# Attention output with queries on the partitions, other estimates for the order of issue, and one ring for the split activations of an FFN

## The chip, the cores and the metric

The kernel runs on one core of one Trainium2 chip. The metric is device time in microseconds (us), from the first to the last instruction of one execution with what lies around it; the time of a kernel is the median of several executions. TensorE is called PE, VectorE DVE, ScalarE ACT, GpSimd POOL, and SyncE (whose queue issues the transfers) SP.

## The reference, cut

Two layers of three residual blocks over 256 tokens of width 1024, each behind an RMSNorm: a SwiGLU feed-forward block (FFN) at half weight, a token mixer of three head groups in parallel, and a second such FFN; then a last RMSNorm.

```python
D_MODEL, SEQ, DEPTH, D_FF = 1024, 256, 2, 2816
MLA_HEADS = 6;  FOX_HEADS = 6            # 12 heads of causal attention, values of 64 channels
def swiglu(h, w_gu, w_down):
    g, u = h @ w_gu                      # two halves, D_FF each
    return (silu(g) * u) @ w_down
def hybrid_mixing(h, ...):
    z = h @ w_in
    ya = mla_mixer(...)      # low-rank q and kv, each with a norm of its own; 64 + 32 rotated channels
    yb = pool_mixer(...)     # causal means over windows of 2, 4, 8 and 16
    yc = fox_mixer(...)      # attention with c[t] - c[s] added to the scores, c = cumsum(log_sigmoid(f))
    return concat([ya, yb, yc]) @ w_out
def reference(x, ...):
    for l in range(DEPTH):
        x = x + 0.5 * swiglu(rmsnorm(x, ffn1_norm[l]), ...)
        x = x + hybrid_mixing(rmsnorm(x, mix_norm[l]), ...)
        x = x + 0.5 * swiglu(rmsnorm(x, ffn2_norm[l]), ...)
    return rmsnorm(x, final_norm)
```

## The kernel before, in words

**Products.** All of `x` stays in SBUF, transposed: channels on the partitions, 256 tokens along the free axis, 8 chunks. A product with a weight is done in three fp32r matmuls: the weight is split in a rounded half `hi` and a rest `lo`, and so is the activation (`hT` holds both halves of the normed input, chunk by chunk; `ph` and `pl` are those of an FFN's middle activation and of the mixer's output). The three are hi by hi, hi by lo and lo by hi, L230 to L232, with the weight stationary and 256 tokens moving. In the last FFN the down product is turned round, so that tokens end on the partitions: there `ph` and `pl` are stationary and the weight moves (L237 to L239). SP loads raw weights in packs of 128x1024; ACT casts them to `hi` (L328), DVE subtracts to `lo` (L343), into 8 places each.

**An FFN** has 22 blocks of 128 middle channels. Each has a gate and an up group of 24 matmuls (8 chunks by three) and a down block of 24 (8 chunks of output by three). The gate is scaled with the norm's factor `R` on DVE (L588), passes a SiLU on ACT (L592), is multiplied by up on DVE (L602), and `split_out` makes `ph` on ACT (L370) and `pl` on DVE (L373). `ffn_order` puts the down block of a middle block LAG = 2 pairs of groups behind its own; the last H = 4 down blocks stand at the end. `ph` and `pl` come from `ptile`: 8 buffers each of 288 floats, of which 256 are used, from an offset that goes round the four values of SKEW. The mixer takes its 8 pairs of output tiles `ys` from the same buffers.

**A norm** is not put ahead of its product: the product runs on unnormed `hT`, and the factor is applied behind it. The factor's chain is: squares, a sum over the partitions on PE (L452, a column per 128 tokens), DVE adds epsilon (L456), POOL takes the power -0.5 (`rsqrt`, L364), PE spreads the factor over the partitions (L465), ACT copies it to `R` (L470). Gate groups cannot leave their banks before `R` is there.

**A mixer** starts with `mix_head` (low-rank inputs and forget gates). Then, as tasks: `lowrank` (transposes, split) and `qkv` (L223 to L225, 36 matmuls); `gates`, which makes the log gates `lf` on ACT and POOL; `decay`, which sums them over time on PE (L243 on `cs` and `lf`), copies the sum to `pc`, and fills the other halves of the tiles `fqk` on DVE (L958, four per head pair); `chunks` (q and k of the fox heads, and the pooling input), with `fox_evac` (L931, L932) into `fqk`; `q_evac` with the rotation of `qf` (`rope`, L820 to L823); `mla_T`, transposes (L247) into `mt`. `attn` runs for each of six head pairs per layer: scores with queries on the partitions (L243), `softmax` on DVE and ACT, the exponentials `e` scaled by the inverse of their sums (L1025 to L1027), three transposes to `pTs`, and the weighted values with v stationary, so that the output has channels on the partitions, as `mix_out` wants it; ACT and DVE split it straight into `yh` and `yl` (L996, L1001), each head on its own half of the partitions. Three PSUM banks of eight belong to a head pair.

**The order** on each engine is fixed when the program is built. Every piece of work is a generator that yields a time (or an event, or a number of banks) and a rank; the class `Issue` keeps a clock per engine, adds an estimated duration for each instruction and LAT for each hop between engines, and lets the ready task of lowest rank go first (L141 to L157). So an estimate that changes reorders instructions everywhere.

```python
    def on(self, eng, cost, *after):      # L112: a clock of estimates, not of the chip
        t = max(self.clk[eng], self.now ...) + cost
    def rsqrt(m, n, key): ...
        return r, q.on("POOL", 0.48)
    def ptile(nm):                        # L534
        o = SKEW[turn[nm] % len(SKEW)]
        return sp.tile([P, 288], F32R, tag=nm, bufs=8, name=nm)[:, o:o + 256]
```

## Time and profile before

| | |
|---|---|
| time, median of 3 executions | 959.35 us (958.14 to 959.65) |
| the profiled execution | 959.65 us, of which the span is 957.9 us |
| PE busy | 933.4 us, 97% |
| DVE busy | 625.2 us, 65% |
| ACT busy | 502.5 us, 52% |
| POOL busy | 56.1 us, 6% |
| transfers | 54% of the 16 DMA engines' time |

The busy time of PE is drawn from the start of a matmul to its modelled end; matmuls overlap, so a busy PE need not be at its peak pace. The pace is read from the starts of the instructions in the timeline, and PE's idle time from the view of its waits, which names the line and the engine that ended each wait.

### The profile page before, as it was taken

To read this page: it belongs to the slowest core of one execution; us is meant where nothing else is said; L and a number is where in the kernel's file an instruction comes from. 1 tells how busy PE (TensorE), PEld (TensorE's weight loads), DVE (VectorE), ACT (ScalarE), POOL (GpSimd) and SP (SyncE) were. 2 spreads that over 40 slices of the span, in tenths; PEclk is the share of its full clock that TensorE was granted. 3 is DMA by queue.
4 is the path that set the end of the run, shared out by engine and by line. 5 is a ranking of instruction groups with operands and counts; after the bars stand their busy time and mean duration, and the time that the engine had idled before them with its cause. 6 is when DMAs were issued, how large, how long until landed. Compare 5 with 4: busy or idle time off the path is not lost.

```text
span 957.9 us, 18788 instructions
## 1 busy us (share of the span) xinstructions
PE 933.4 (97%) x7788; PEld 921.4 (96%) x7788; DVE 625.2 (65%) x1018; ACT 502.5 (52%) x797; POOL 56.1 (6%) x104
## 2 busy tenths in 40 slices
PE   8999999998999999999999999999989999999997
PEld 7999999997989999999999999999988999999997
DVE  6755555568996755555686555557599676555553
ACT  6544444456664644444465444445565665444442
POOL 1000000022210000000000000000504000000000
PEclk9999999999999999999999999999999999999999
DMA  7776656422463766565556566652524557555631
GB/s 258 242 256 196 193 192 188 157 86 96 144 192 109 259 199 198 198 198 185 169 170 212 192 198 198 196 178 75 173 73 140 191 160 258 196 184 194 197 113 44
DMA packets 48326, 168.95 MB, mean 176 GB/s; under 512 B 5360, under 2 KB 5744, under 8 KB 48240
## 3 DMA queue, kind: packets, MB, share of 16 engines
q1 hardware_dynamic: 48096, 167.66, 54.0%
q8 instruction: 61, 1.00, 0.4%
q14 instruction: 25, 0.20, 0.1%
q10 hardware_dynamic: 144, 0.09, 0.0%
HBM read 166.68 MB, written 1.05 MB: 175 GB/s over the span
## 4 chain that ended last, share of the span: by engine, by line
PE 84%; DVE 9%; POOL 2%; issue 1%; DMA 1%; ACT 1%; SPq 0%; POOLq 0%; DVEq 0%; ACTq 0%
PE bank L231 24%; PE bank L230 24%; PE bank L232 24%; DVE lo L343 2%; PE bank L239 2%; PE bank L237 2%; PE bank L238 2%; PE bank L243 1%; PE bank L223 1%; PE bank L225 1%; PE bank L224 1%; DVE fqk L958 1%; PE bank L247 1%; POOL rsn L364 1%; DVE sm L1012 1%
## 5 line engine op out<-in xcount | busy, mean ns | idle before, releaser
L343 DVE TENSOR_TENSOR lo<-raw,hi 128x1024 fp32r<-128x1024 f32 (+3 forms) x320 | 382.7, 1204 | 180.3 <-ACT hi L328 179.4
L230 PE MATMUL bank<-hT,hi 128*128 128x256 f32 x1536 | 430.2, 280 | 0.0
L232 PE MATMUL bank<-hT,lo 128*128 128x256 f32 x1536 | 426.4, 278 | 0.7 <-DVE lo L343 0.4
L231 PE MATMUL bank<-hT,hi 128*128 128x256 f32 x1536 | 426.2, 277 | 0.0
L328 ACT CAST hi<-raw 128x1024 fp32r<-128x1024 f32 (+3 forms) x320 | 328.6, 1030 | 161.1 <-PE bank L231 105.1
L232 PEld LDWEIGHTS bank<-hT,lo 128*128 128x128 f32 x1536 | 289.4, 188 | 1.5 <-DVE lo L343 1.5
L230 PEld LDWEIGHTS bank<-hT,hi 128*128 128x128 f32 x1536 | 289.5, 188 | 0.7 <-ACT hi L328 0.4
L231 PEld LDWEIGHTS bank<-hT,hi 128*128 128x128 f32 x1536 | 289.5, 188 | 0.3
L230 PE MATMUL bank<-ph,hi 128*128 128x256 f32 x656 | 183.8, 280 | 0.0
L231 PE MATMUL bank<-pl,hi 128*128 128x256 f32 x656 | 182.6, 278 | 0.8 <-DVE pl L373 0.8
L232 PE MATMUL bank<-ph,lo 128*128 128x256 f32 x656 | 182.2, 278 | 0.0
L231 PEld LDWEIGHTS bank<-pl,hi 128*128 128x128 f32 x656 | 123.2, 188 | 1.1 <-DVE pl L373 1.0
L230 PEld LDWEIGHTS bank<-ph,hi 128*128 128x128 f32 x656 | 123.3, 188 | 0.1
L232 PEld LDWEIGHTS bank<-ph,lo 128*128 128x128 f32 x656 | 123.2, 188 | 0.0
L592 ACT ACTIVATE s<-s 128x256 f32<-128x256 f32 x88 | 36.5, 418 | 150.7 <-DVE s L588 150.7
L588 DVE TENSOR_TENSOR s<-bank,R 128x256 f32<-128x256 f32 x88 | 37.2, 424 | 39.0 <-PE bank L232 36.2
L373 DVE TENSOR_TENSOR pl<-p,ph 128x256 fp32r<-128x256 f32 x88 | 37.2, 425 | 37.7 <-ACT ph L370 37.7
L370 ACT CAST ph<-p 128x256 fp32r<-128x256 f32 x88 | 35.6, 407 | 27.8 <-DVE p L602 27.6
L237 PE MATMUL bank<-lo,ph 128*128 128x256 f32 x176 | 49.3, 280 | 0.0
L239 PE MATMUL bank<-hi,ph 128*128 128x256 f32 x176 | 49.2, 280 | 0.0
L238 PE MATMUL bank<-hi,pl 128*128 128x256 f32 x176 | 49.2, 279 | 0.0
L364 POOL TENSOR_TENSOR rsn<-m,mhalf 128x2 f32<-128x2 f32 x6 | 9.2, 1536 | 642.1 <-DVE m L456 642.1
(143 smaller groups left out, 755.6 us busy)
## 6 DMA issues: line engine op xcount, KB each, us to landing
raw<-wpk SPq DMA_DIRECT2D x294, 512.0 KB, 4.1
raw<-wpk SPq DMA_DIRECT2D x16, 403.0 KB, 3.1
raw<-wpk SPq DMA_DIRECT2D x4, 288.0 KB, 3.7
x<-xin SPq DMA_DIRECT2D x4, 256.0 KB, 5.6
raw<-wpk SPq DMA_DIRECT2D x4, 256.0 KB, 5.7
out<-h SPq DMA_DIRECT2D x4, 256.0 KB, 2.2
raw<-wpk SPq DMA_DIRECT2D x2, 384.0 KB, 4.2
cs<-cst SPq DMA_DIRECT2D x1, 582.0 KB, 6.7
```

The lines of the kernel that those rows point to most:

```text
L230: T.matmul(o, lhsT=hi, rhs=xh, start=start, stop=False, skip_group_check=True)
L231: T.matmul(o, lhsT=hi, rhs=xl, start=False, stop=False, skip_group_check=True)
L232: T.matmul(o, lhsT=lo, rhs=xh, start=False, stop=stop, skip_group_check=True)
L237: T.matmul(o, lhsT=lh, rhs=rl, start=start, stop=False, skip_group_check=True)
L238: T.matmul(o, lhsT=ll, rhs=rh, start=False, stop=False, skip_group_check=True)
L239: T.matmul(o, lhsT=lh, rhs=rh, start=False, stop=stop, skip_group_check=True)
L328: A.copy(h[:, :w], r[:, :w])
L343: V.tensor_tensor(out=lo[:, :w], in0=r[:, :w], in1=h[:, :w].bitcast(F32), op=ALU.subtract)
L370: A.copy(dh, src)
L373: V.tensor_tensor(out=dl, in0=src, in1=dh.bitcast(F32), op=ALU.subtract)
L588: V.tensor_tensor(out=s, in0=b[:, 0:256], in1=g.nm.R, op=ALU.mult)
L592: A.activation(s, s, AF.Silu)
```

## The change

**The weighted values are turned round.** In `attn` the transposed exponentials are now stationary and 64 columns of v move, so that queries are on the partitions of the output. The sums' inverse is taken in a task of its own (`inverse`) and applied to the output in one DVE product of 128x256, in place of the scaling of the exponentials ahead of their transposes. Two transposes bring the scaled output `y` back to channels on the partitions, into the free half of the same bank, and `split_out` splits it, both heads in one instruction per engine.

**Estimates.** PE's fp32r rate 2245 in place of 2185, LAT 0.2 in place of 0.15, POOL's power 1.4 in place of 0.48 for two columns and other POOL costs, 0.42 for a fill (L958), and the end of an exponential 0.9.

**LAG** is 3 in place of 2. **The ring:** `ph` and `pl` of a block lie side by side in one of 8 places behind `hT`, in one tile `hb`, taken from the last place to the first; the place used by blocks 0, 8 and 16 is moved on by SKEW = 12 floats. `ys` uses the same places.

```diff
-LAG = 2
+LAG = 3
-SKEW = [28, 16, 16, 16]
+RING = 8
+SKEW = 12
-    LAT = 0.15
+    LAT = 0.2
-        return q.on("PE", 3 * 256 / 2185.0)
+        return q.on("PE", 3 * 256 / 2245.0)
...
-    hT = cp.tile([P, KC, 2, 256], F32R, name="hT")
+    hb = cp.tile([P, (KC + RING) * 512 + 64], F32R, name="hb")
+    hT = hb[:, 0:KC * 512].rearrange("p (k s t) -> p k s t", k=KC, s=2)
...
-        return r, q.on("POOL", 0.48)
+        return r, q.on("POOL", 1.4 if n > 1 else 0.55)
...
-    def ptile(nm):
-        o = SKEW[turn[nm] % len(SKEW)]
-        turn[nm] += 1
-        return sp.tile([P, 288], F32R, tag=nm, bufs=8, name=nm)[:, o:o + 256]
+    def ring(n):
+        n = RING - 1 - n % RING
+        o = (KC + n) * 512 + (SKEW if n == RING - 1 else 0)
+        return hb[:, o:o + 256], hb[:, o + 256:o + 512]
...
-        ph, pl = ptile("ph"), ptile("pl")
+        ph, pl = ring(fc)
...
-            self.ys = [(ptile("ph"), ptile("pl")) for _ in range(8)]
+            self.ys = [ring(n) for n in range(8)]
...
-        q.on("POOL", 0.4)
+        q.on("POOL", 1.3)
-        t = q.on("POOL", 0.55)
+        t = q.on("POOL", 1.3)
-        t = max(t, q.on("POOL", 0.7))
+        t = max(t, q.on("POOL", 0.35))
...
-                    t = dve(256, fast=True)
+                    t = q.on("DVE", 0.42)
...
         for h in range(2):
             yield res[h][0], R_ATT
             pt = res[h][1]
-            c0 = h * 256
-            mm(o[:, c0:c0 + 256], v[:, 0, j * P:(j + 1) * P], pt[:, 0:256], True, False)
-            t = mm(o[:, c0 + P:c0 + 256], v[:, 1, j * P:(j + 1) * P], pt[:, 256:384], False, True)
+            for tb in range(2):
+                w = slice(tb * P + 64 * h, tb * P + 64 * h + 64)
+                for k in range(tb + 1):
+                    c0 = (tb + k) * P
+                    t = mm(o[:, w], pt[:, c0:c0 + P], v[:, k, j * P + 64 * h:j * P + 64 * h + 64], k == 0, k == tb)
         g.ev_att[n].set(t)
         yield t + LAT, R_EVAC
+        y = sp.tile([P, 256], F32, tag="y", bufs=2, name="y")
+        V.tensor_tensor(out=y.rearrange("p (a d) -> p a d", a=4), in0=o[:, 0:256].rearrange("p (a d) -> p a d", a=4),
+                        in1=rc.rearrange("p a h -> p (a h)").unsqueeze(2).to_broadcast([P, 4, 64]), op=ALU.mult)
+        t = dve(256)
+        yield t + LAT, R_TP
+        for tb in range(2):
+            t = tr(o[:, 256 + tb * P:256 + (tb + 1) * P], y[:, tbs(tb)])
+        yield t + LAT, R_EVAC
         yh, yl = g.ys[c]
-        for h in range(2):
-            r = slice(64 * h, 64 * h + 64)
-            A.copy(yh[r], o[r, h * 256:(h + 1) * 256])
-            t = act(256)
-        yield t + LAT, R_EVAC
-        for h in range(2):
-            r = slice(64 * h, 64 * h + 64)
-            V.tensor_tensor(out=yl[r], in0=o[r, h * 256:(h + 1) * 256], in1=yh[r].bitcast(F32), op=ALU.subtract)
-            t = dve(256)
+        t = yield from split_out(yh, yl, o[:, 256:512])
         q.give(o, t + LAT)
...
-        t = act(384, acc=0.3)
-        yield t + LAT, R_CHAIN
-        rc = small(2, "rc")
-        V.reciprocal(rc, sums)
-        V.tensor_scalar(out=e[:, 0:P], in0=e[:, 0:P], scalar1=rc[:, 0:1], scalar2=None, op0=ALU.mult)
-        V.tensor_scalar(out=e[:, P:384], in0=e[:, P:384], scalar1=rc[:, 1:2], scalar2=None, op0=ALU.mult)
-        t = q.on("DVE", 0.67)
+        t = q.on("ACT", 0.9)
+        q.spawn(inverse(rc, sums, t + LAT))
         yield t + LAT, R_TP
...
+    def inverse(rc, sums, t):
+        yield t, R_EVAC
+        V.reciprocal(rc, sums)
+        q.on("DVE", 0.08)
```

What the estimates and the turned values do to the order is seen at three places. In the rows below a line number is followed by the operation, out<-in, the tile's shape, and a count where the same stands several times in a row; lines of the kernel after are one to three higher.

PE at the start of layer 0's second FFN, from the sum of squares (`sf`) to the spreading of the factor (`rsn`), before:

```order
L452 MATMUL bank_74<-one,sf 128x1 x2
L230 MATMUL bank_69<-hT,hi_3687 128x256
L231 MATMUL bank_69<-hT,hi_3687 128x256
L232 MATMUL bank_69<-hT,lo_3752 128x256
...
L465 MATMUL bank_71<-fs,rsn 128x128 x2
```

The same place after:

```order
L454 MATMUL bank_67<-one,sf 128x1 x2
L231 MATMUL bank_71<-hb,hi_3621 128x256
L232 MATMUL bank_71<-hb,hi_3621 128x256
L233 MATMUL bank_71<-hb,lo_3686 128x256
...
L231 MATMUL bank_71<-hb,hi_3644 128x256
L232 MATMUL bank_71<-hb,hi_3644 128x256
L233 MATMUL bank_71<-hb,lo_3716 128x256
L467 MATMUL bank_70<-fs,rsn 128x128 x2
```

Between the two stand nine matmuls of a first gate group before, and eighteen after.

DVE in layer 0's mixer, from the first decay fills (L958, `fqk`) to the first rotation (L823, `qf`), before:

```order
L958 TENSOR_SCALAR fqk_2738<-pc,cs 64x256 x2
L958 TENSOR_SCALAR fqk_2739<-pc,cs 64x256 x2
L219 TENSOR_SCALAR qf<-bank_67,lr_2614 128x288
L931 TENSOR_TENSOR fqk_2738<-bank_69,R 64x256
L932 TENSOR_TENSOR fqk_2738<-bank_69,R 64x256
L958 TENSOR_SCALAR fqk_2758<-pc,cs 64x256 x2
L958 TENSOR_SCALAR fqk_2759<-pc,cs 64x256 x2
L820 TENSOR_TENSOR r_2774<-qf,cs 128x192
L821 TENSOR_TENSOR r_2775<-qf,cs 128x6x16
L822 TENSOR_TENSOR r_2775<-qf,cs 128x6x16
L823 TENSOR_TENSOR qf<-r_2774,r_2775 128x6x32
```

The same place after, where the fills are L960, the rotation ends at L825, and `mt` is the copy behind the MLA transposes:

```order
L220 TENSOR_SCALAR qf<-bank_67,lr_2624 128x288
L822 TENSOR_TENSOR r_2728<-qf,cs 128x192
L823 TENSOR_TENSOR r_2729<-qf,cs 128x6x16
L824 TENSOR_TENSOR r_2729<-qf,cs 128x6x16
L825 TENSOR_TENSOR qf<-r_2728,r_2729 128x6x32
L960 TENSOR_SCALAR fqk_2749<-pc,cs 64x256 x2
L960 TENSOR_SCALAR fqk_2750<-pc,cs 64x256 x2
L212 COPY mt_2773<-bank_72 96x512
L933 TENSOR_TENSOR fqk_2749<-bank_71,R 64x256
L934 TENSOR_TENSOR fqk_2749<-bank_71,R 64x256
L933 TENSOR_TENSOR fqk_2750<-bank_73,R 64x256
L934 TENSOR_TENSOR fqk_2750<-bank_73,R 64x256
```

The first rotation stood behind eight of the twelve fills and one product of a fox chunk, and stands ahead of them all.

PE in layer 0's mixer around the decay sum (`cs`, `lf`), before, where L223 to L225 on `qkh` and `qkl` are the low-rank projections:

```order
L230 MATMUL bank_74<-hT,hi_2572 128x256
L231 MATMUL bank_74<-hT,hi_2572 128x256
L232 MATMUL bank_74<-hT,lo_2641 128x256
L243 MATMUL bank_68<-cs,lf_86 128x256
L243 MATMUL bank_68<-cs,lf_87 128x128
L223 MATMUL bank_73<-lo_2694,qkh 128x288
L224 MATMUL bank_73<-hi_2623,qkl 128x288
L225 MATMUL bank_73<-hi_2623,qkh 128x288
```

The same place after, where the projections are L224 to L226:

```order
L226 MATMUL bank_68<-hi_2628,qkh 128x384
L224 MATMUL bank_70<-lo_2642,qkh 128x384
L225 MATMUL bank_70<-hi_2628,qkl 128x384
L226 MATMUL bank_70<-hi_2628,qkh 128x384
L231 MATMUL bank_73<-hb,hi_2502 128x256
L232 MATMUL bank_73<-hb,hi_2502 128x256
L233 MATMUL bank_73<-hb,lo_2531 128x256
L244 MATMUL bank_74<-cs,lf_86 128x256
L244 MATMUL bank_74<-cs,lf_87 128x128
L231 MATMUL bank_73<-hb,hi_2502 128x256
```

The decay sum stood ahead of the 36 matmuls of the projections, behind a fox chunk, and stands behind them, inside the next chunk.

## Rows read from the trace of the kernel before

**Rows 1.** Page parts 1 and 2: engine totals; granted clock in 40 slices.

```profile
PE 933.4 (97%) x7788; PEld 921.4 (96%) x7788; DVE 625.2 (65%) x1018; ACT 502.5 (52%) x797; POOL 56.1 (6%) x104
...
PEclk9999999999999999999999999999999999999999
```

**Rows 2.** Waits of PE: line waited for: us in total, times, longest.

```profile
PE bank L465 <- POOL rsn L364: 4.0, 4, 1.4
PE bank L247 <- DVE qf L823: 3.4, 2, 1.7
PE bank L243 <- POOL lf L806: 2.7, 2, 1.4
PE bank L247 <- ACT pTs L209: 1.4, 2, 0.7
...
PE bank L243 <- DVE pl L1001: 0.8, 2, 0.4
PE bank L247 <- DVE e L1027: 0.8, 2, 0.4
PE bank L231 <- DVE pl L373: 0.8, 1, 0.8
```

**Rows 3.** Timeline, PE, first FFN: start us, drawn us, line, operation, operands.

```profile
28.23 0.28 PE L230 MATMUL bank<-hT,hi 128*128 128x256 f32 x1
...
31.05 0.28 PE L230 MATMUL bank<-ph,hi 128*128 128x256 f32 x1
...
33.87 0.28 PE L230 MATMUL bank<-hT,hi 128*128 128x256 f32 x1
...
39.31 0.28 PE L230 MATMUL bank<-ph,hi 128*128 128x256 f32 x1
...
42.14 0.28 PE L230 MATMUL bank<-hT,hi 128*128 128x256 f32 x1
...
47.59 0.28 PE L230 MATMUL bank<-ph,hi 128*128 128x256 f32 x1
...
50.31 0.28 PE L230 MATMUL bank<-hT,hi 128*128 128x256 f32 x1
```

**Rows 4.** Timeline, PE, second FFN, after its norm.

```profile
323.99 0.28 PE L230 MATMUL bank<-ph,hi 128*128 128x256 f32 x1
...
326.81 0.28 PE L230 MATMUL bank<-hT,hi 128*128 128x256 f32 x1
```

**Rows 5.** Timeline, PE, last FFN, where `ph` and `pl` are stationary.

```profile
843.01 0.28 PE L237 MATMUL bank<-lo,ph 128*128 128x256 f32 x1
...
845.73 0.28 PE L230 MATMUL bank<-hT,hi 128*128 128x256 f32 x1
...
851.39 0.28 PE L237 MATMUL bank<-lo,ph 128*128 128x256 f32 x1
...
854.22 0.28 PE L230 MATMUL bank<-hT,hi 128*128 128x256 f32 x1
...
856.95 0.28 PE L230 MATMUL bank<-hT,hi 128*128 128x256 f32 x1
```

**Rows 6.** Chain of waits, layer 0's mixer: start us, us, what, count.

```profile
238.74 1.84 PE bank L247 x15
240.58 3.93 PE bank L243 x24
```

**Rows 7.** Timeline, PE, norm ahead of the mixer: narrow fp32 matmuls.

```profile
203.29 0.28 PE L452 MATMUL bank<-one,sf 128*128 128x1 f32 x2
...
205.93 0.38 PE L465 MATMUL bank<-fs,rsn 128*128 128x128 f32 x2
```

**Rows 8.** Timeline, DVE, layer 0's mixer; in brackets the idle time before.

```profile
222.06 0.42 DVE L958 TENSOR_SCALAR fqk<-pc,cs 64x256 f32<-64x256 f32 x1 [2.30 <-ACT pc L209]
...
230.44 0.69 DVE L211 COPY mt<-bank 96x512 f32<-96x512 f32 x1
```

**Rows 9.** Windows, start: stretch, us, busy (count) of five engines, clock, DMA, GB/s.

```profile
18.00:21.00 3.00, 2.98 (x16) 2.99 (x17) 1.58 (x3) 2.24 (x5) 0.00 (x0) 0.60 0.90 288
```

More of the change, by code (lines that the diff above doesn't have):

```diff
@@ L197, in trunk, with dve @@
         q.free.append((0.0, ps.tile([P, 512], F32, tag=f"bank{i}", name=f"bank{i}")))
-    def dve(n, *after, fast=False):
-        return q.on("DVE", 0.07 + n / (1920.0 if fast else 960.0), *after)
+    def dve(n, *after):
+        return q.on("DVE", 0.07 + n / 960.0, *after)
     def act(n, *after, acc=0.0):
@@ L225, in mm3 @@
         T.matmul(o, lhsT=lh, rhs=rh, start=False, stop=stop)
-        return q.on("PE", 3 * int(np.prod(rh.shape[1:])) / 2185.0, *after)
+        return q.on("PE", 3 * int(np.prod(rh.shape[1:])) / 2245.0, *after)
     def mmw(o, hi, lo, xh, xl, start, stop):
@@ L239, in mm3w @@
         T.matmul(o, lhsT=lh, rhs=rh, start=False, stop=stop, skip_group_check=True)
-        return q.on("PE", 3 * 256 / 2185.0)
+        return q.on("PE", 3 * 256 / 2245.0)
     def mm(o, lhsT, rhs, start, stop, *after):
@@ L529, in final @@
             nc.sync.dma_start(out[tb, :, c], h)
-    turn = {"ph": 0, "pl": 0}
-    def ptile(nm):
-        o = SKEW[turn[nm] % len(SKEW)]
-        turn[nm] += 1
-        return sp.tile([P, 288], F32R, tag=nm, bufs=8, name=nm)[:, o:o + 256]
+    def ring(n):
+        n = RING - 1 - n % RING
+        o = (KC + n) * 512 + (SKEW if n == RING - 1 else 0)
+        return hb[:, o:o + 256], hb[:, o + 256:o + 512]
     class F:
@@ L774, in lowrank_rms @@
         G.tensor_scalar(out=g.lr[tb], in0=rs, scalar1=r, scalar2=None, op0=ALU.mult)
-        g.ev_r[tb].set(q.on("POOL", 0.2) + LAT)
+        g.ev_r[tb].set(q.on("POOL", 0.3) + LAT)
     def gates(g, tb, bB, t):
@@ L977, in attn @@
         res = [[Ev(), None], [Ev(), None]]
+        rc = small(4, "rc", bufs=3).rearrange("p (a h) -> p a h", a=2)
         for h, b in ((0, b0), (1, b1)):
@@ L980, in attn @@
             t = mm(b[:, P:384], qt[0:kk, h, P:256], kt[0:kk, h, :], True, True)
-            q.spawn(softmax(b, t, scale, res[h]))
+            q.spawn(softmax(b, t, scale, res[h], rc[:, :, h]))
             yield t, R_ATT
```

2 lines of the change are left out of this document (1 added, 1 removed).

## The prediction

> **What bounds the kernel now.** I read the page first. TensorE (PE) is busy 933.4 of 957.9 us [rows 1], so any gain is either PE time without work, which is 24.5 us in all, or matmuls that follow each other more closely. Then I read who PE waits for [rows 2]. A row there is total idle, number of waits, longest wait. Three kinds matter: four waits for the factor of a norm (`rsn`, from GpSimd), one for the first `pl` of an FFN, and ten inside the two mixers. Idle is counted from the drawn end of a matmul; a matmul is drawn 0.28 us long while the next one starts 0.113 us after it [rows 3], so a wait costs 0.17 us more than its row says. Last I read start times, because the mean duration of a matmul doesn't show its pace. The profiled execution took 959.65 us for a span of 957.9 us; the median of the runs is 959.35, 0.3 less. The sum is made as gains on the profiled execution and taken off the median.
>
> **The pace of the matmuls.** Each row of [rows 3] is the first of 24 matmuls in a row (one gate or up group, or one down block). The group at 28.23 takes 2.82 us, the down block at 31.05 takes 2.82, the two groups after it 5.44 together, the block at 39.31 takes 2.83, and the block at 47.59 takes 2.72. So there are two paces, 2.72 and 2.82 us per 24, while the granted clock is at its higher level throughout [rows 1]. What goes with them is where the moving operand lies. In the built program all halves of `hT` start 64 bytes past a multiple of 256. The `ph` and `pl` buffers are 1,152 bytes apart, so they alternate between 64 and 192, and every fourth is pushed on by 48 more bytes. The block at 39.31 is a 192, that at 47.59 a 64, that at 31.05 a 112. A 64 after a fast group is fast; a 192 is slow; after a 112 or a 192 the next group is fast again. The pace also sticks: the block at 323.99 is a 64 in a slow stretch and takes 2.82 [rows 4].
>
> **The ring.** All ring places lie at 64, as `hT` does, but the one for down blocks 0, 8 and 16 of an FFN, which lies at 112. For FFNs 1 to 3: before, eight blocks in a row lie at 112, 192, 64, 192, 240, 64, 192, 64; at 0.10 to 0.11 us for each that isn't 64 (the 240 is between, 0 to 0.11) that is 0.4 to 0.5 per eight, 1.35 per FFN of 22 blocks. After, three blocks cost 0.10 each: gain 1.05 per FFN, 3.2 for three. The slow stretch after each norm ends at down block 0, which now comes one pair of groups later: 2 x 0.10 x 3 = 0.6 lost. The output projection of the mixers reads the same buffers, much broken up by attention: 0.3 gained. In the last FFN `ph` and `pl` are the stationary operand. There a 64 at 843.01 takes 2.72, the two groups after it 5.66, the next 64 at 851.39 takes 2.83, and only the group after that, at 854.22, is fast again with 2.73 [rows 5]. With nearly all blocks at 64 this would go on in pairs: two groups slowed (0.22) for one fast block (0.11), 0.1 lost per pair of blocks, half of ten pairs if the 112s break the series: 0.5 lost. Sum: 3.2 - 0.6 + 0.3 - 0.5 = **2.4 us gained**; ends 0 and 4.
>
> **Norms.** PE puts matmuls between the sum of squares (L452) and the matmul that spreads the factor (L465). The planner now charges 1.4 instead of 0.48 for the GpSimd power, and the order has 9 more matmuls there at each of the four FFN starts (3 to 12, 9 to 18, 9 to 18; 6 to 15 in the last). The four waits cost 4.0 + 4 x 0.17 = 4.7 [rows 2]; 9 matmuls cover 9 x 0.114 = 1.03 each: **4.0 gained**, ends 3.0 and 4.7. No work is added: these matmuls stood behind the wait. What is then late is the chain factor, gate, up, `pl`, first down block. LAG 3 puts 48 more matmuls (5.5 us) ahead of that block, so the one wait for `pl` (0.8 + 0.17) goes as well: **1.0 gained**, ends 0.5 and 1.0.
>
> **Mixers, what is added.** Each of 12 head pairs gets two transposes; 15 take 1.84 us in the chain [rows 6], so 24 take 2.9. The weighted values become six 64-column fp32 matmuls, 12 records, instead of four matmuls in 8 records, which take 8/24 of 3.93 = 1.31 [rows 6]. No 64-column fp32 matmul is in the trace. Four records of one column are drawn over 0.50, four of 128 columns over 0.60 [rows 7]; less 0.17 of drain that is 0.08 and 0.11 each, 1.0 to 1.3 for 12. I take no change, as for 128 columns, with -0.3 per pair as the other end. The VectorE work that is dropped (scaling the exponentials) and that is added (scaling the output, one row-wide product) is not on PE; it counts only by the waits below.
>
> **Mixers, what is moved.** The five kinds of wait in [rows 2] (`qf`, `lf`, `pTs`, `pl` L1001, `e`) sum to 9.1, ten waits, 10.8 with 0.17 each. By the new order: (1) The wait for `lf` goes: the decay matmuls now stand behind all 36 matmuls of the low-rank projections instead of ahead of them, more than 4 us of cover for 1.4. (2) The wait for `qf` goes: VectorE does both rotations first and the eight decay fills (L958) after, 2 x 1.70 us [rows 8] that were ahead of the second. (3) A new one appears: the first scores need, after the decay matmuls, a copy on ScalarE, four fills (1.70), a copy of `mt` (0.69) [rows 8] and four products of the fills' shape (1.70 again), with hops 4.8; PE has 24 matmuls and 8 transposes in between, 3.7: wait 1.1. (4) A transpose of the second MLA pair needs a bank that VectorE frees behind four maxima: 0.7 as I follow the queues. (5) The first output scaling stands behind a weight split on VectorE: 0.2. Behind that I find each chain covered, since VectorE has 0.7 us less to do per head. With 0.3 for what I missed: 2.3 per layer, 4.6 in all; ends 1 and 11. Gain 10.8 - 4.6 - 2.9 = **3.3 us**, ends 8 gained and 3 lost.
>
> **Sum:** 2.4 + 4.0 + 1.0 + 3.3 = 10.7; 959.35 - 10.7 = **948.6 us**.
>
> **Rivals.** (a) *The waits move.* Each head pair's end is now longer by a scaling, two transposes and a split, holding its PSUM bank, so the mixers may wait as long as before: 10.8 stay. For it: the estimates say little about banks. Against: the stalls of [rows 2] all have their releaser moved ahead in the queues. Then 2.4 + 4.0 + 1.0 - 2.9 = 4.5: 954.8.
> (b) *The place of the operand does nothing* and the two paces come from something else that went along with it. Then the ring's 2.4 is 0: 951.0. Against: [rows 3] repeat with the buffers, 39.31 and 47.59 being neighbours of one loop. [...]
> (c) *Slower: the slow pace sticks.* Without the 192s, only the three 112s of an FFN can end a slow stretch. If a 112 does not, every FFN from its norm on runs like 323.99 [rows 4]: 66 groups x 0.10 = 6.6 us for each of three FFNs, 19.8, less the 5.6 lost there before (1.35 in the down blocks, 0.5 ahead of the first), 14.2 worse: 959.35 - 8.3 + 14.2 = 965.3. It decides the sign once some 70% of the groups are slow. For it: [rows 4]. Against: in [rows 3] the 112 at 31.05 comes from slow groups and leaves fast ones.
> [...]
>
> **Chances and range.** Forecast 0.62, (a) 0.15, (b) 0.08, (c) 0.05, (d) 0.10. The range 943.5 to 954.5 leaves out (c), half of (a) and a part of (d). A measurement of this kernel can tell about 0.2%, 1.9 us, from no change: all but (c) and the far end of (a) are faster by more: faster 0.93, same 0.03, slower 0.04.
>
> **What would show it.** Norms: the row L465 for `rsn` under 0.8 in all, no wait for `pl` before the first down block. Ring: down blocks of 2.72 in FFNs 1 to 3 but for numbers 0, 8 and 16; in the last FFN pairs of slow groups. Mixers: no waits for `lf` or `qf`, one of about 1 us for `fqk`. I would be wrong above all if groups of 2.82 fill an FFN, or if PE's waits in a mixer sum to more than 5 us.

## The result, and the profile after

The kernel after takes 945.15 us (median of 4, 944.66 to 945.8) where the kernel before took 958.75 in the same comparison (4 runs, 958.0 to 959.65): a ratio of 0.9856, interval 0.9844 to 0.9867. The gain is 13.6 us by the medians, 15.0 between the two profiled executions (959.65 and 944.66) and 15.9 between their spans (957.9 and 942.0); what lies around the span grew from 1.8 to 2.7 us. The forecast was 948.6, a gain of 10.7.

Page part 1 of the kernel after, as in [rows 1]:

```profile
PE 929.1 (99%) x7860; PEld 920.9 (98%) x7860; DVE 608.6 (65%) x972; ACT 497.6 (53%) x783; POOL 62.4 (7%) x104
```

PE is busy 4.3 us less in a span that is 15.9 shorter: its idle time fell from 24.5 to 12.9 us. The waits of PE after, columns as in [rows 2]:

```profile
PE bank L248 <- DVE fqk L934: 1.6, 2, 0.8
...
PE bank L248 <- ACT e L1026: 0.7, 4, 0.2
...
PE bank L467 <- POOL rsn L366: 0.3, 1, 0.3
```

The row for the norms' factor fell from 4.0 to 0.3; only the first FFN's norm still waits. The rows for `lf`, `qf`, `pTs`, `pl` and for the scaled `e` are gone. New are 0.8 per mixer for `fqk` and four short waits for `e`, now released by ACT. Behind the first norm the clock does not drop in this execution; the window that answers to [rows 9], same columns:

```profile
18.00:21.00 3.00, 2.92 (x25) 2.93 (x26) 2.37 (x4) 2.44 (x5) 0.02 (x1) 1.00 0.89 277
```

The granted clock was 0.60 there before, and is 1.00. Last the pace. The timeline of PE in the first FFN after, each row the first of 24 matmuls as in [rows 3]; the down block at 33.61 is number 0, at 112, the one at 41.87 is number 1, at 64:

```profile
33.61 0.28 PE L231 MATMUL bank<-hb,hi 128*128 128x256 f32 x1
...
36.41 0.28 PE L231 MATMUL bank<-hb,hi 128*128 128x256 f32 x1
...
41.87 0.28 PE L231 MATMUL bank<-hb,hi 128*128 128x256 f32 x1
...
44.59 0.28 PE L231 MATMUL bank<-hb,hi 128*128 128x256 f32 x1
```

2.80 us for the 112, 5.46 for the two groups behind it, and 2.72 for the 64. The whole span by stages, from each norm's sum (L452, in after L454) to the next, from the starts in both traces: the first three FFNs are 4.1, 3.6 and 2.7 us shorter, the two mixers 2.5 and 3.0, the last FFN 0.0; matmuls that the new order moved across a boundary are counted back (1.1 us of each mixer's head, 2.0 between the second and the third FFN). The sum is 15.9.

### The profile page after: what moved, and what is told of

Read it like the earlier page. It is cut to its first block, busy times and chain, and to the rows that moved or that the text cites. A ratio compares the mean times of both kernels' runs of the same rounds, so it can differ in the third digit from the quotient of the medians.

```text
span 942.0 us, 18948 instructions
## 1 busy us (share of the span) xinstructions
PE 929.1 (99%) x7860; PEld 920.9 (98%) x7860; DVE 608.6 (65%) x972; ACT 497.6 (53%) x783; POOL 62.4 (7%) x104
## 4 chain that ended last, share of the span: by engine, by line
PE 95%; DVE 2%; ACT 1%; issue 1%; DMA 1%; POOL 0%; SPq 0%; POOLq 0%; DVEq 0%
PE bank L231 26%; PE bank L233 26%; PE bank L232 26%; PE bank L244 3%; PE bank L238 2%; PE bank L240 2%; PE bank L239 2%; PE bank L248 2%; PE bank L224 2%; PE bank L225 2%; PE bank L226 2%; DMA x<-xin 1%; DVE fqk L960 0%; PE bank L467 0%; DVE fqk L934 0%
## 5 line engine op out<-in xcount | busy, mean ns | idle before, releaser
L231 PE MATMUL bank<-hb,hi 128*128 128x256 f32 x2192 | 613.7, 280 | 0.0
L233 PE MATMUL bank<-hb,lo 128*128 128x256 f32 x2192 | 608.1, 277 | 0.6 <-DVE lo L345 0.5
L232 PE MATMUL bank<-hb,hi 128*128 128x256 f32 x2192 | 607.7, 277 | 0.0
L231 PEld LDWEIGHTS bank<-hb,hi 128*128 128x128 f32 x2192 | 413.0, 188 | 0.5 <-ACT hi L330 0.2
L233 PEld LDWEIGHTS bank<-hb,lo 128*128 128x128 f32 x2192 | 411.8, 188 | 1.5 <-DVE lo L345 1.5
L232 PEld LDWEIGHTS bank<-hb,hi 128*128 128x128 f32 x2192 | 411.9, 188 | 0.3
L375 DVE TENSOR_TENSOR hb<-p,hb 128x256 fp32r<-128x256 f32 x88 | 37.2, 425 | 37.6 <-ACT hb L372 37.5
L372 ACT CAST hb<-p 128x256 fp32r<-128x256 f32 x88 | 35.4, 406 | 26.4 <-DVE p L604 26.0
L238 PE MATMUL bank<-lo,hb 128*128 128x256 f32 x176 | 49.1, 279 | 0.0
L239 PE MATMUL bank<-hi,hb 128*128 128x256 f32 x176 | 49.0, 278 | 0.0
L240 PE MATMUL bank<-hi,hb 128*128 128x256 f32 x176 | 49.0, 278 | 0.0
L604 DVE TENSOR_TENSOR p<-bank,s 128x256 f32<-128x256 f32 x88 | 36.5, 419 | 11.2 <-PE bank L233 10.2
L238 PEld LDWEIGHTS bank<-lo,hb 128*128 128x128 f32 x176 | 33.1, 188 | 0.0
L240 PEld LDWEIGHTS bank<-hi,hb 128*128 128x128 f32 x176 | 33.1, 188 | 0.0
L239 PEld LDWEIGHTS bank<-hi,hb 128*128 128x128 f32 x176 | 33.0, 188 | 0.0
```

What stands on the lines that cost most here:

```text
L231: T.matmul(o, lhsT=hi, rhs=xh, start=start, stop=False, skip_group_check=True)
L232: T.matmul(o, lhsT=hi, rhs=xl, start=False, stop=False, skip_group_check=True)
L233: T.matmul(o, lhsT=lo, rhs=xh, start=False, stop=stop, skip_group_check=True)
L238: T.matmul(o, lhsT=lh, rhs=rl, start=start, stop=False, skip_group_check=True)
L239: T.matmul(o, lhsT=ll, rhs=rh, start=False, stop=False, skip_group_check=True)
L240: T.matmul(o, lhsT=lh, rhs=rh, start=False, stop=stop, skip_group_check=True)
```

## The experiments

Each kernel was timed beside the kernel before on the same chip; the median of before lay between 958.75 and 959.64, so ratios are compared. After has 0.9856. Differences by the spans are between the two profiled executions.

### The ring

**ring_192**: all places of the ring 128 bytes further.

```diff
-        o = (KC + n) * 512 + (SKEW if n == RING - 1 else 0)
+        o = (KC + n) * 512 + 32 + (SKEW if n == RING - 1 else 0)
```

> The kernel after, with every place of the ring moved by 128 bytes: seven places lie at 192 past a multiple of 256, the eighth at 240; the order of issue and the work are the same. Theory 'place' (the pace of a matmul is set by where its moving operand lies): in the kernel before, the down block at 39.31 lay at 192 and took 2.83 us where the 64 at 47.59 took 2.72, so 22 blocks of each of three FFNs lose 0.1 each, 6.6 us, less 0.9 that the nine 112s lose already: about 5.5 us slower than after, 950.7. The mixers could gain part of it, 2 us at most, since their slow stretch at 272 to 300 us of the trace of after would be broken by 192s. So 948.5 to 951. Theory 'place does nothing': within 0.5 us of 945.15.

950.18 us (949.34 to 950.42), ratio 0.9899 (0.9884 to 0.9914): 4.1 us slower than after. PE in the first FFN, a down block at 192, the group behind it, and the start of the next:

```profile
41.60 0.28 PE L231 MATMUL bank<-hb,hi 128*128 128x256 f32 x1
...
44.43 0.28 PE L231 MATMUL bank<-hb,hi 128*128 128x256 f32 x1
...
47.16 0.28 PE L231 MATMUL bank<-hb,hi 128*128 128x256 f32 x1
```

2.83 for the block and 2.73 for the group. The work and the order are those of after, so where the operand lies does count, and rival (b) falls. The mixers' slow stretch was not broken up; their part of the expectation did not come.

**ring_no_skew**: all places at 64.

```diff
-SKEW = 12
+SKEW = 0
```

> The kernel after, with SKEW = 0: all eight places at 64. 'Place': the nine down blocks at 112 become fast, 0.09 us each, 0.8 us gained in FFNs 0 to 2. 'Sticky' (a slow stretch ends only at a place other than 64): a stretch that a wait turned slow has nothing left to end it; in the mixers the slow stretch of after ran from 272 to the next norm at 300 us, 0.108 us per 24 matmuls, and would begin earlier; where an FFN begins slow it stays so, 66 groups, 7 us. In after FFNs 0 and 1 begin fast without help, so 944.4 without stickiness in FFNs, 951 to 958 if one or two FFNs stay slow. 'Place does nothing': 945.15.

Six runs: 940.69, 940.87, 946.43, 954.65, 956.39, 957.15. One program, one order, and 16 us between its runs, while after stays within 1.1 in its four. All six count here, since the scatter is what is tested; the granted clock does not account for it, since it was 0.996 in the run of 940.87 and in that of 956.39. The profiled run (954.65) has two of its first three FFNs slow from end to end, and the third fast. PE in the first FFN, a group and a down block, then a group in the third:

```profile
40.78 0.28 PE L231 MATMUL bank<-hb,hi 128*128 128x256 f32 x1
...
43.60 0.28 PE L231 MATMUL bank<-hb,hi 128*128 128x256 f32 x1
...
46.43 0.28 PE L231 MATMUL bank<-hb,hi 128*128 128x256 f32 x1
...
497.71 0.28 PE L231 MATMUL bank<-hb,hi 128*128 128x256 f32 x1
...
500.43 0.28 PE L231 MATMUL bank<-hb,hi 128*128 128x256 f32 x1
```

2.82 and 2.83 us in the first FFN, 2.72 in the third, with every `hT`, `ph` and `pl` at 64 in both. The pace is a state that sticks: in these two FFNs, which have no odd place, nothing ended it, and each is 7 us longer for it. So the state that rival (c) feared is real. The best of these runs is 4 us faster than after, whose nine 112s in the first three FFNs cost 0.8 us in all. Where the rest lies isn't shown, since that run has no trace; the profiled run has 2.6 us less of slow pace than after in the mixers and the last FFN.

**no_ring**: after with the buffers of before.

```diff
-        ph, pl = ring(fc)
+        ph, pl = ptile("ph"), ptile("pl")
-            self.ys = [ring(n) for n in range(8)]
+            self.ys = [(ptile("ph"), ptile("pl")) for _ in range(8)]
-        y = sp.tile([P, 256], F32, tag="y", bufs=2, name="y")
+        y = sp.tile([P, 512], F32, tag="dx", bufs=3, name="y")[:, 0:256]
```

> The kernel after with the ph and pl buffers of before (8 of each, 1,152 bytes apart, at 112, 192, 64, 192, 240, 64, 192, 64) in place of the ring; the scaled output y lies in the buffers of dx for lack of room. LAG, estimates, turned values as in after. 'Place': by the starts of the matmuls the ring gave 5.1 us in FFNs 0 to 2, took 2.0 in the two mixers and 1.0 in the last FFN, so this kernel is 2.1 us slower than after: 947.3. 'Place does nothing': 945.15.

946.87 us (946.33 to 949.13), ratio 0.987 (0.9856 to 0.9885): 1.3 us slower than after, with intervals that overlap, so the times alone don't show a gain. The spans of the profiled runs differ by 2.6 us (944.54 and 941.96).

**ring_alone**: before with the ring.

```diff
-        ph, pl = ptile("ph"), ptile("pl")
+        ph, pl = ring(fc)
-            self.ys = [(ptile("ph"), ptile("pl")) for _ in range(8)]
+            self.ys = [ring(n) for n in range(8)]
```

> The kernel before with the ring alone (LAG 2, old estimates, old attention). If the ring is worth what its account in the trace says, and that doesn't hang on the other parts: 2.1 us faster than before, 956.6. 'Sticky': in before each FFN began in a slow stretch behind the wait for its norm, until the first down block at 112 ended it; here the first down block lies at 112 too, so it should end there: no loss. If a 112 does not end it: 6.6 us for each FFN, up to 970. 'Place does nothing': 958.75.

957.47 us (ten runs, 955.79 to 962.11), ratio 0.9989 (0.9973 to 1.0004): 1.1 us by the ratio, no difference that can be told. The profiled run (961.78) has most of its second FFN slow, behind the waits that the old order still has. PE there: a group, down block 8 (at 112), and the next group; then the group behind down block 16, which is at 112 too:

```profile
379.50 0.28 PE L231 MATMUL bank<-hb,hi 128*128 128x256 f32 x1
...
382.32 0.28 PE L231 MATMUL bank<-hb,hi 128*128 128x256 f32 x1
...
385.14 0.28 PE L231 MATMUL bank<-hb,hi 128*128 128x256 f32 x1
...
452.97 0.28 PE L231 MATMUL bank<-hb,hi 128*128 128x256 f32 x1
...
455.69 0.28 PE L231 MATMUL bank<-hb,hi 128*128 128x256 f32 x1
```

2.82 and 2.82, and the group at 385.14 is as slow; but the group behind block 16 takes 2.72. Of the five 112s in the first three FFNs of this trace that came in a slow stretch, three ended it (block 0 in the first and in the third FFN, block 16 here) and two did not (blocks 0 and 8 here). So a 112 ends a slow stretch often, not always.

### Estimates, turned values, LAG

**estimates_alone**: before with the new estimates only.

```diff
-    LAT = 0.15
+    LAT = 0.2
-        return r, q.on("POOL", 0.48)
+        return r, q.on("POOL", 1.4 if n > 1 else 0.55)
-                    t = dve(256, fast=True)
+                    t = q.on("DVE", 0.42)
...
```

> The kernel before with the new estimates alone (LAT 0.2, 2245, the POOL costs, 0.42 for a fill); LAG 2, old buffers, old attention. The order then has 9 to 9 more matmuls inside the norms of the four FFNs, as in after. Theory 'order' (most of the gain is waits that the new order covers): the waits for the norms' factor (4.7 us with what a wait costs beside its row) and the low clock behind the first of them (1.2) go, and so do those for lf and qf in the mixers (7.0 in four waits by the starts of the matmuls); new waits for fqk, about 1 per mixer, come. 10 us faster than before, 949 where before is 959.2. Theory 'attention' (the mixers' waits went because the turned attention leaves DVE 0.7 us less work per head): the mixers keep their waits and only the norms gain, 6 us: 953.

959.7 us (ten runs, 957.85 to 963.02), ratio 1.0008 (0.9998 to 1.0019). Neither forecast came: no gain at all. The waits of PE:

```profile
PE bank L247 <- DVE fqk L932: 4.3, 2, 2.2
PE bank L247 <- DVE e L1026: 3.3, 4, 1.5
PE bank L230 <- ACT ph L370: 1.5, 1, 1.5
PE bank L247 <- ACT pTs L209: 1.4, 2, 0.8
```

The rows for the norms, `lf` and `qf` did go, as foretold. But 1.5 us came back ahead of a first down block, and in the mixers the waits for `fqk` and for the scaled `e` grew to 4.3 and 3.3. With `pTs` that is 9.0, where the five kinds of [rows 2] sum to 9.1: the mixers wait as long as before, under other names. The granted clock fell behind them; the window of the first mixer (columns as in [rows 9]):

```profile
235.00:242.00 7.00, 6.42 (x27) 5.57 (x27) 4.26 (x9) 3.69 (x11) 0.00 (x0) 0.54 0.25 77
```

0.54, where after has 1.00 in the same stretch: fp32 matmuls of 256 columns that took 0.22 us each took 0.43 there, about twice as long. Over whole runs it was 0.985 to 0.991 in these ten, and 0.995 to 0.997 in the runs of before beside them. The mixers were 3.1 and 2.4 us longer than before, with the matmuls that the order moved ahead of them counted back, and used up what the FFNs gained.

**turned_alone**: before with the new `attn`, `softmax` and `inverse`, y in the buffers of dx; estimates, LAG and buffers of before.

```diff
-            mm(o[:, c0:c0 + 256], v[:, 0, j * P:(j + 1) * P], pt[:, 0:256], True, False)
-            t = mm(o[:, c0 + P:c0 + 256], v[:, 1, j * P:(j + 1) * P], pt[:, 256:384], False, True)
+                    t = mm(o[:, w], pt[:, c0:c0 + P], v[:, k, j * P + 64 * h:j * P + 64 * h + 64], k == 0, k == tb)
...
```

> The kernel before with the turned attention alone (queries on the partitions of the output, two transposes more per head pair, scaling of the output; y in the buffers of dx), old estimates, LAG 2, old buffers. 'Order': 24 transposes at 0.11 add 2.6 us; the waits for pTs, pl and e (0.84, 0.31, 0.31 and 0.58 per mixer beyond a matmul's pace, 4.1 in both) may go with the shorter VectorE queue; from 1.5 us faster to 2.6 slower, taken 0.5 slower than before. 'Attention': 4 us faster or more.

954.19 us (953.44 to 954.47), ratio 0.9943 (0.9927 to 0.996): 5.5 us faster than before, more than either end of the first theory. The waits of PE:

```profile
PE bank L465 <- POOL rsn L364: 4.1, 4, 1.4
PE bank L247 <- DVE qf L823: 3.4, 2, 1.7
PE bank L243 <- POOL lf L806: 2.7, 2, 1.4
```

What the order makes stayed (4.1, 3.4, 2.7, as in [rows 2]); what the attention makes (`pTs`, `pl`, `e`) is gone, and the two mixers are 2.8 us shorter each by the starts, the new transposes counted in.

**scaled_early**: after with the exponentials scaled on DVE ahead of their transposes, and y a plain copy.

```diff
-        q.spawn(inverse(rc, sums, t + LAT))
+        yield t + LAT, R_CHAIN
+        rc = small(2, "rc")
+        V.reciprocal(rc, sums)
+        V.tensor_scalar(out=e[:, 0:P], in0=e[:, 0:P], scalar1=rc[:, 0:1], scalar2=None, op0=ALU.mult)
+        V.tensor_scalar(out=e[:, P:384], in0=e[:, P:384], scalar1=rc[:, 1:2], scalar2=None, op0=ALU.mult)
+        t = q.on("DVE", 0.67)
...
-        V.tensor_tensor(out=y.rearrange("p (a d) -> p a d", a=4), in0=o[:, 0:256].rearrange("p (a d) -> p a d", a=4),
-                        in1=rc.rearrange("p a h -> p (a h)").unsqueeze(2).to_broadcast([P, 4, 64]), op=ALU.mult)
+        V.tensor_copy(y, o[:, 0:256])
```

> The kernel after with the exponentials scaled by the inverse of their sums on DVE ahead of their transposes, as before; the output is copied to y unscaled, so that PE, ACT and the way of the output (values turned, two transposes, split) stay as in after; DVE has 0.6 us more per head, in the chain from the exponentials to the transposes. Theory 'chain' (the mixers gained because that chain became shorter): waits for e come back, 0.7 us in four waits in after against 3.3 in four in the kernel with the estimates alone, with what they bring in pace and clock: 3 to 6 us slower than after, 948 to 951, ratio 0.989 to 0.992. Theory 'output' (they gained because the output's split is shorter and its bank comes free sooner): within 1 us of after, ratio 0.985 to 0.987.

956.84 us (ten runs, 952.64 to 961.1), ratio 0.9979 (0.9958 to 1.0): 11.8 us slower than after by the ratio, 8.0 by the spans of the profiled runs (950.0 and 942.0). The two mixers are 3.8 and 4.4 us longer, the rest is as in after. The clock is part of it: over whole runs it was 0.993 in the three shortest (952.64 to 952.82, the profiled one among them), 0.983 to 0.985 in the four longest (958.67 to 961.1), and 0.996 to 0.998 in after. The chain decides, not the output, and it decides more than either theory had. The waits of PE:

```profile
PE bank L248 <- DVE fqk L934: 4.3, 2, 2.2
PE bank L248 <- ACT pTs L210: 1.7, 2, 0.8
```

The waits came back under other names than I had expected. In both kernels a transpose of `qf` needs the bank that the second product of `fox_evac` (L934) frees at 231.5. PE around it, first after, then scaled_early (start us, drawn us, line, operation, count, idle before and what ended it):

```profile
229.20 0.91 PE L248 MATMUL bank<-fs,e 128*128 128x128 f32 x4
...
230.27 0.44 PE L248 MATMUL bank<-fs,e 128*128 128x128 f32 x2 [0.16 <-ACT e L1026]
...
231.52 0.64 PE L248 MATMUL bank<-fs,qf 128*96 128x128 f32 x4 [0.81 <-DVE fqk L934]
```

```profile
231.44 0.64 PE L248 MATMUL bank<-fs,qf 128*96 128x128 f32 x4 [2.16 <-DVE fqk L934]
...
231.96 1.36 PE L248 MATMUL bank<-fs,e 128*128 128x128 f32 x6
```

In after PE puts six transposes of `e` ahead of it, which need only ACT's exponentials, and waits 0.81. In scaled_early these transposes wait for DVE, which is busy with four heads' maxima and the fox product until 231.4 and then scales; they come after 231.96, and PE stands still for 2.16. What this run can't part is the shorter chain from the order that goes with it, since the planner puts the transposes in another place when the scaling stands ahead of them.

**lag2**: after with LAG = 2.

```diff
-LAG = 3
+LAG = 2
```

> The kernel after with LAG = 2. If the third pair is what covers the chain from the norm's factor to the first pl: the factor is spread 9 matmuls later than before, so the first down block waits 1 to 2 us at each FFN whose norm waits cover nothing more, 1 to 4 us slower than after (946 to 949). If the chain was covered anyway: the same as after within 0.5 us.

948.38 us (947.33 to 955.54), ratio 0.9901 (0.9864 to 0.9939): 4.3 us slower by the ratio, 3.8 by the spans. One wait came back, in the second FFN, and behind it the clock (window as in [rows 9]):

```profile
PE bank L231 <- ACT hb L372: 1.9, 1, 1.9
```

```profile
305.00:316.00 11.00, 8.98 (x62) 8.59 (x61) 9.19 (x13) 7.58 (x11) 0.00 (x0) 0.84 0.85 288
```

1.9 us of wait and 11 us at a clock of 0.84; the second FFN is 4.1 us longer than in after. One of the four runs took 955.54 at a clock of 0.993 and pulls the ratio up; it has no trace, and a slow FFN as in ring_no_skew would be of that size. The other three lie between 947.33 and 949.14. So the third pair of groups covers the chain from the norm's factor to the first `ph`, which starts later now that the factor is spread later.

**power_048**: after with the old estimate for POOL's power.

```diff
-        return r, q.on("POOL", 1.4 if n > 1 else 0.55)
+        return r, q.on("POOL", 0.48)
```

> The kernel after with the old estimate, 0.48, for POOL's power alone. The order has 3, 9, 9 and 10 matmuls inside the FFNs' norms, as before. 'Order': four waits of 1 us come back, 4.7, and the low clock behind the first norm, 1.2; FFNs then start at the slow pace behind a wait, until the 112 of the first down block: 0.5 each. 6 us slower than after, 951. If the wait only moves to another place of the chain (the gate group cannot leave its bank before the factor anyway): under 2 us.

948.46 us (947.7 to 951.65), ratio 0.9892 (0.9874 to 0.9911): 3.5 us slower. The norms' waits came back in full:

```profile
PE bank L467 <- POOL rsn L366: 4.8, 6, 1.4
```

Six waits, 4.8 us, in place of one of 0.3: four in the FFNs and two at the mixers' norms, where before had none. The low clock behind the first norm is back too (window as in [rows 9]):

```profile
18.00:21.00 3.00, 3.00 (x17) 3.00 (x18) 2.05 (x3) 2.17 (x5) 0.00 (x0) 0.63 0.95 303
```

The slow starts that I expected with them did not come: the three FFNs have no more of the slow pace than in after. And the mixers have 1.2 us less each in the sum of matmul intervals that is used in the next section, which is about the 2.5 us by which I missed. The run is not about the FFNs' norms alone: this estimate also counts in the mixers, where the order changed, the wait for `fqk` is gone, and `e` waits 2.2 us where after has 0.7.

### The two operands

**kick_192**: the odd place at 192, and read last in each closing pass of a mixer.

```diff
-SKEW = 12
+SKEW = 32
-            self.ys = [ring(n) for n in range(8)]
+            self.ys = [ring(n + 1) for n in range(8)]
```

> The kernel after with the ring's one odd place at 192 in place of 112 (SKEW 32), and with the mixers' output tiles taken one place on, so that the odd place is read last in each of the four passes at the end of a mixer; nothing else is changed. 'Sticky' (a stretch that became slow stays slow until an operand at another place ends it, and a 192 ends it each time, as in ring_192): the slow stretch from 272 to 300 us in each mixer is ended by the first pass, 1.0 us gained per mixer, the FFNs stay as they are, 2 us faster than after: 943.1 where after is 945.15, ratio 0.9836 to before. 'Place does nothing': the same as after, ratio 0.9856.

Eight runs, median 945.04: five from 943.97 to 945.26, three from 950.79 to 957.11; ratio 0.9888 (0.9846 to 0.9929). No gain that can be told, and a scatter like that of ring_no_skew is back. In the profiled run the closing stretch of the first mixer is fast; its block of 24, then the one that answers to it in after:

```profile
275.78 0.28 PE L231 MATMUL bank<-hb,hi 128*128 128x256 f32 x1
...
278.50 0.28 PE L231 MATMUL bank<-hb,hi 128*128 128x256 f32 x1
```

```profile
274.85 0.28 PE L231 MATMUL bank<-hb,hi 128*128 128x256 f32 x1
...
277.68 0.28 PE L231 MATMUL bank<-hb,hi 128*128 128x256 f32 x1
```

2.72 against 2.83, 0.9 us over that mixer, as the theory had it. The second mixer kept its slow stretch and is 1.5 us longer than in after, and the first FFN 1.0 us longer: in both the granted clock dropped where after has 1.00, with PE in the same order and behind waits as short. The window behind the first norm (as in [rows 9]), then the one in the second mixer:

```profile
18.00:21.00 3.00, 3.00 (x20) 3.00 (x19) 1.81 (x3) 1.93 (x5) 0.02 (x1) 0.64 0.91 274
690.00:695.00 5.00, 3.88 (x20) 2.98 (x21) 3.73 (x12) 3.60 (x13) 0.00 (x0) 0.76 0.11 14
```

What the three longer runs did can't be seen, since they have no trace.

**weights_64** and **weights_192**: all weight buffers moved by 192 and by 64 bytes, so that they lie at 64 and at 192 where after has 128; hT and the ring keep their places, and the tiles behind the weights keep theirs counted modulo 256 bytes.

```diff
-    hb = cp.tile([P, (KC + RING) * 512 + 64], F32R, name="hb")
+    hb = cp.tile([P, (KC + RING) * 512 + 112], F32R, name="hb")
...
```

(80 in place of 112 for weights_192.)

> The kernel after with all weight buffers moved by 192 bytes, so that they too lie at 64 (before: 128); the ring and the other tiles keep their places. In the last FFN the weights move, and after each of its down blocks the pace of the gate and up groups changes over (slow, fast, slow). If that is the place of the moving weights: down blocks and groups keep one pace, the 112 of the first down block makes it the fast one, 3 us faster than after, and the 48 wide matmuls at the head of each mixer may gain up to 0.6 us per mixer: 941 to 942.5, ratio 0.982 to 0.983. If what counts is the distance between the stationary and the moving operand, all gate and up groups of the kernel change with it: up to 7 us slower per FFN. 'Place does nothing': ratio 0.9856.

> The kernel after with all weight buffers moved by 64 bytes, so that they lie at 192, 128 bytes from hT and the ring (64); in after the distance is 64 the other way, in weights_64 it was 0 and every group took 2.88 us. Theory 'distance' (the pace is set by how the stationary and the moving operand lie to each other, not by where the moving one lies): every gate, up and down group of the kernel has another pace than in after, one and the same for all 64s, and it doesn't change over in the last FFN, where the two operands change roles at the same distance of 128. How fast cannot be said from the runs: 2.72 or less per group throughout would take 10 us off after (935), 2.82 throughout adds 18 us (963). Theory 'place of the moving operand': gate and up groups stay as in after; only the last FFN changes, by 4 us at most: 941 to 949.

983.7 us (980.81 to 983.92), ratio 1.0247, and 973.29 us (972.58 to 977.1), ratio 1.0143. In the first FFN, a group and the down block behind it, of weights_64 and of weights_192:

```profile
48.66 0.28 PE L231 MATMUL bank<-hb,hi 128*128 128x256 f32 x1
...
51.54 0.28 PE L231 MATMUL bank<-hb,hi 128*128 128x256 f32 x1
...
54.42 0.28 PE L231 MATMUL bank<-hb,hi 128*128 128x256 f32 x1
```

```profile
49.34 0.28 PE L231 MATMUL bank<-hb,hi 128*128 128x256 f32 x1
...
52.19 0.28 PE L231 MATMUL bank<-hb,hi 128*128 128x256 f32 x1
...
55.03 0.28 PE L231 MATMUL bank<-hb,hi 128*128 128x256 f32 x1
```

2.88 us each in the one, 2.85 and 2.84 in the other, in gate, up and down blocks alike, and in the last FFN too, where nothing changes over any more. The moving operand lies where it lay; only the stationary one was moved, and every group changed its pace. So the pace belongs to the pair, and the reading that fits all these runs is how the stationary and the moving operand lie to each other. At 64 bytes one way (after) there are two states, 2.72 and 2.82, and at 0 and 128 bytes one, slower than both.

## Why the prediction was right, and where its reasons were not

The time lay in the range, 3.5 us under the forecast. That it falls on 945.1, the time that went with rival (d), a larger gain, is luck. (d) had two terms beside the forecast: 1.2 us for the low clock behind the first norm (0.60 over 3 us [rows 9], so 3 x 0.4) came, at least in the profiled execution; 2.3 us, for half of the forecast mixer waits, did not: 2.1 per mixer are left where the forecast had 2.3. Step by step:

**Norms: right for the waits; (d)'s clock is not settled.** 4.0 + 1.0 were forecast. By the starts, the intervals over 0.1 us too long in the four FFNs fell from 6.9 to 0.9 us, a gain of 6.0. Some 0.6 of it is the low clock behind the first norm, which I had put in rival (d) and not in the forecast; in all that clock cost 1.7 (0.60 over 3 us [rows 9], so 1.2, and 0.5 more over the next 3 at 0.83), and the other part stands in the sum of the next paragraph. That the nine matmuls in that wait keep the clock up, on which (d) counted, is not shown: ring_no_skew, lag2, kick_192 and weights_192 have the order of after at this norm, and in each of their traces the granted clock from 15 to 21 us is 0.72, where after has 1.00. It falls there sooner than in before, behind the wait of 1.3 us for the sum of squares, which all these kernels have. power_048 takes 3.5 of the gain back, lag2 3.8 by the spans: each alone loses more than half of it, since either leaves one of the two ends of the same chain open. Costing them as two separate terms was a simplification that the sum forgave.

**Ring: the size not told by the times, the account wrong in part.** 2.4 were forecast. no_ring gives 1.3 by its ratio, with intervals that overlap, and 2.6 by its span; what follows is read from one trace of each. I add up, over all 256-column matmuls of a stage, the part of each interval over 0.1133 us (2.72 / 24), and leave intervals that are more than 0.1 longer to the waits. The first three FFNs went from 6.8 to 1.7 us in after. no_ring has 5.2, so 3.5 is the ring's. Of the other 1.6, 0.9 is the low clock behind the first norm, whose intervals of about 0.2 us are no slow pace, and 0.7 comes from FFNs that no longer start behind a wait (I had a loss of 0.6 there). The mixers went from 4.5 to 6.5, where I had a gain of 0.3; no_ring has 6.6, so that isn't the ring's. 1.1 of these 2.0 isn't pace either: where the fp32r matmuls are taken up again behind others, the first interval is about 0.2 us, and a mixer has 18 of these after where it had 12 before, which belongs to the new stream of attention. The rest is slow pace, and a matter of the state: lag2 has the same attention and the same ring, and 1.0 less of it in its first mixer. The last FFN went from 3.3 to 4.4. A loss of 0.5 was forecast, by pairs of slow groups, and they are there; but no_ring has 4.1 without the ring, so only 0.3 of the loss is the ring's. PE in the last FFN after, as in [rows 5]; L238 is a down block:

```profile
781.82 0.28 PE L238 MATMUL bank<-lo,hb 128*128 128x256 f32 x1
...
784.54 0.28 PE L231 MATMUL bank<-hb,hi 128*128 128x256 f32 x1
...
787.37 0.28 PE L231 MATMUL bank<-hb,hi 128*128 128x256 f32 x1
...
790.20 0.28 PE L238 MATMUL bank<-lo,hb 128*128 128x256 f32 x1
...
793.03 0.28 PE L231 MATMUL bank<-hb,hi 128*128 128x256 f32 x1
```

2.72 for the down block, 2.83 and 2.83 for the two groups behind it, 2.83 for the next block.

**The cause behind the ring was only half right.** "The place of the moving operand" held only because the weights never moved: weights_64 and weights_192 show that it is the place of both. And rival (c), at 0.05, deserved more. Its state exists and costs up to 7 us an FFN (ring_no_skew; some 5.5 in ring_alone); that after escapes it may come from FFNs that begin without a wait, or from the 112s. Which of the two is not shown: ring_alone has 112s with and without effect, ring_no_skew FFNs that stay slow without one. Four runs of after that agree don't show that it always escapes.

**Mixers, what is added: forecast too high by about 1.** 2.9 were forecast for 24 transposes and nothing for the turned values. By the starts, each to the next, the 24 transposes of `y` take 2.1 us and the values 0.2 less than before; all transposes and fp32 matmuls of both mixers, intervals over 0.33 us left out, take 1.0 more. The six values of one pair take 1.28 us for 12 records (the first group here, to the start of the second):

```profile
234.41 1.45 PE L244 MATMUL bank<-vm,pTs 128*128 128x64 f32 x12
...
235.69 0.83 PE L244 MATMUL bank<-vf,pTs 128*128 128x64 f32 x6
```

That is the 1.31 of before, as for 128 columns.

**Mixers, what is moved: a sum on the right side by the wrong cause.** 6.2 us of waits less were forecast. By the intervals over 0.33 us, less what the instruction takes without a wait, they fell from 12.1 to 4.1, so 8.0 went; left are 2.1 per mixer, where I had 2.3. By the stages the two mixers are 5.5 us shorter, where I had 3.3. Of the new ones, (4), the bank behind the maxima, came with 0.8 for 0.7; (3) and (5) did not come, four short waits for `e` did. So the sign "one of about 1 us for `fqk`" came true by (4) and not by (3), for which it stood. But I had derived all this from the order, and called the turned attention a cost of 2.9 with "0.7 us less to do per head" on DVE as a remark at the end. The experiments say otherwise. The order without the turned attention gains nothing (estimates_alone, 1.0008): it moves the rotation and the decay sum out of the way, and the waits return as `fqk` and `e`, with a low clock. The turned attention without the order gains 5.5 us (turned_alone), and putting only the scaling back into the chain costs 8 us or more (scaled_early). So rival (a), that the waits move, is what the order alone does; what keeps them from moving is that transposes of `e` no longer stand behind DVE, with the order that this allows. The step that failed is that (1) to (5) were costed from the order: the dropped VectorE work, which "counts only by the waits below", has no term there and is brought in at the end. With the new order and the old attention the rows of the mixers' waits sum to 9.0 us, where before has 9.1.

**What stays open.** Why the FFNs of after begin fast behind their norms, while those of ring_no_skew, with the same order, begin either way; why the mixers' closing stretch is slow in after and fast in the first mixer of lag2; and why the clock drops behind the same waits in one execution and not in another. Of a kernel faster than after there is only the best of ring_no_skew, 940.69, which its other runs don't hold; kick_192 was the attempt at it and failed.

## What to carry to other kernels

Before costing a wait by what is ahead of it in the order, ask which engine's queue the released work still has to pass: work that is not on the bottleneck engine can still cost a good part of its duration when it stands in a busy engine's chain (here 0.75 us of DVE for each of 24 heads, 18 us in all, were worth 8 us of the whole), and a better order may show its worth only together with it. Read the pace of equal matmuls from their starts; where it has two values, compare the places of both operands, and run such a kernel many times, since one profile shows only one of its states; the same holds for a clock that did or didn't drop.

## What the runs showed of the hardware

- The same 24 matmuls (256 columns, fp32r) took 2.72, 2.82, 2.83, 2.85 or 2.88 us in the profiled runs, whose granted clock was 0.993 to 0.998 over the whole, and the times went with the places of the stationary and the moving operand (given modulo 256 bytes; that 256 is the period was not tested): 2.72 or 2.82 at 128 and 64 (after, ring_no_skew), 2.83 at 128 and 192 (ring_192), 2.88 at 64 and 64 (weights_64), 2.85 at 192 and 64 (weights_192), stationary named first. weights_64 and weights_192 move the weights alone, so the place of the stationary operand counts beside that of the moving one; what in the chip makes the difference no run shows.
- At 128 and 64 the two paces are states that stick: with all places of the ring alike, one program had groups of 2.82 us throughout two FFNs and of 2.72 in a third (ring_no_skew, one trace), and ran in 940.69 and in 957.15 us. A down block at 112 ended a slow stretch three times of five (ring_alone).
- Around a wait of PE of 1.9 us the granted clock was 0.84 over 11 us (lag2), and it was 0.54 over the 7 us behind a wait of 2.2, with one of 0.6 among them (estimates_alone): by estimate up to 11 x 0.16 = 1.8 us and 7 x 0.46 = 3.2 us lost, in both about as much again as the waits. It need not be so each time: with the same order and waits of 0.8 at most the granted clock from 690 to 695 us was 0.76 in kick_192 and 1.00 in after.
